# A decoder of two layers on one core: adaLN units moved into layer 1's start and within each mixer's tail, the router's logits copied ahead of the high parts

## The chip, the cores and the metric

The kernel runs on one core of one Trainium2 chip. Its engines are TensorE (PE), VectorE (DVE), ScalarE (ACT), GpSimd (POOL) and SyncE (SP), each with a queue of instructions of its own; SP issues the transfers of the weights. The metric is the device time of one execution in microseconds.

## The reference

A trunk of two layers over 256 tokens of 1024 channels, in f32. Each layer is a token mixer and a mixture of experts, both modulated by adaLN from one conditioning vector `c`:

```python
c_act = jax.nn.silu(c)
for l in range(DEPTH):                                   # 2
    mod = c_act @ ada_w[l] + ada_b[l]                    # (1024) @ (1024 x 6144)
    sh1, sc1, g1, sh2, sc2, g2 = split(mod, 6)
    h = rmsnorm(x, norm_mix_g[l]) * (1 + sc1) + sh1
    proj = h @ w_in[l]                                   # heads of three groups: A, B, C
    oa = differential_attention(...)                     # 4 heads, causal, dense
    ob = banded_attention(..., sink)                     # 8 query heads, window 128
    oc = dilated_mixture(...)                            # 4 heads, three dilations
    x = x + g1 * (concat(oa, ob, oc) @ w_out[l])
    h = rmsnorm(x, norm_ffn_g[l]) * (1 + sc2) + sh2
    x = x + g2 * hierarchical_moe(h, ...)                # best of 4 groups, best 2 of its 4 experts
return rmsnorm(x, final_norm_g)
```

The router's logits are `h @ wg` (4 groups) and `h @ we` (16 experts). An expert is `silu(t @ w_gate) * (t @ w_up)`, weighted, `@ w_down`, with 512 inner channels.

## The kernel before

All 256 tokens stay in SBUF as two tiles `x[0]`, `x[1]` of 128 tokens. What is large is the weights, some 280 MB in all, and they pass through the core once. The class `Ring` holds a ring of 128x1024 tiles (`big`, 512 KB each, and some lent ones, `w` and `k`); `Ring.load` (L154) issues the transfers on SP's queue in one fixed order, which is the order in which TensorE will use them. When the ring is full, the next load waits until the tile that it goes into has been used.

**Order of the work.** TensorE runs its instructions in the order in which the program writes them. The other engines' queues are ordered by a scheduler, which can move an instruction ahead of another one where data and buffers allow; `tc.issue_after` names an instruction that has to come first in the queue. The program's order of a mixer comes from three lists of words, `START`, `MIX` and `TAIL`. `START[l]` is run by `start(l)`, of which layer 1's part is woven into the last expert products of layer 0; `MIX[l]` with `TAIL` at its end is run by `mixer(l)`; then come `router(l)` and `moe(l)`. The words are:

- `X`, `X0` to `X3`: columns of x as it becomes final, transposed (L669). `R`: the inverse norm, as a row product (L680). `S00` to `S02`: splits of the first w_in tiles.
- `P00` to `P43`: pieces of the input projection, each of which uses one w_in tile. An f32 product is made of three products of parts (L718, L719, L720), the high part by ScalarE (L770) and the low part by VectorE (L775), some steps ahead.
- `a`, `c`, `d`, `e`: units of adaLN, a product of `c` and two tiles of `ada_w`. A unit `a` (`ada_unit`, L457, 4 matmuls) belongs to the mixer's shift, scale and gate and the experts' shift (in layer 1, eight units for the last two), a unit `d` or `e` (`one_unit`, L532) to the two halves of what follows the router: four `d` for the second scale, four `e` for the second gate. A unit only adds to a PSUM bank that is read when the last unit is done; what follows it (columns through L475 or L546) is run at the next `flush`.
- `AT AF AV AO AM`, `BT BF BV BO`, `CT CF CV CO`: transposes, scores, values and outputs of the three groups of heads. `CF0` and `CF1` (scores of C, L1074) give their bank to VectorE, which takes the maxima (L829), then ScalarE the exponentials (L835). `CT0` and `CT1` make keys and queries of C (L803; copies L1067 and L1068).
- `W0` to `W6`: output projection, k tile by k tile (`W6` takes the last two), into four banks `acc[t, hf]`. After `W6`, VectorE multiplies by the gate and adds to x (L1141, L1142).

**Router.** `router(l)` transposes x (L803, copies L1180 and L1182), forms raw logits (L1189), has ScalarE copy them (L1195) and adds up their parts (L1196). The inverse norm comes from VectorE's Newton steps (L652 to L660); L1209 multiplies the logits by it. From there VectorE ranks (L1217 to L1229), three small products count places (L1233 to L1235), and L1303 makes the selection matrix `w`. ScalarE scales x to a high part `xhi` (L1206), VectorE forms the low part `xlo` (L1246).

**Experts.** `moe(l)` takes the experts by pairs. `gather` (L1327) collects the chosen tokens by products of `xhi` and `xlo` with the selection matrix; L1361 is the first products (gate and up), L1407 and L1442 the second, L1428 and L1459 the way back to the tokens. A second path of the program, taken when an expert has too many tokens, isn't executed here.

Of the kernel before, what the change touches and what calls it, by code (L numbers as in the profile page):

```python
# [13 lines left out]
AF = mybir.ActivationFunctionType  # L14
# [41 lines left out]

START = ["X c c R c c S00".split(), "S00 S01 X0 X1 S02 X2 X3 a a R".split()]
TAIL = """
CT0 CT1 d d d d CF0 AM1 CF1
W0 BV0 BV1 W1 BV2 BV3 BO0 BV4 W2 BV5 CV0 W3 BO1 CV1 CV2 W4 CO0 W5 W6  # L60
"""
# [6 lines left out]
P00 P01 P02 P03 P10 P11 AT0 P12 AT1 P13 AF0  # L68
P20 a AF1 P21 a AF2 P22 a P23 a
P30 AV0 P31 AV1 a AO0 BT0 P32 AV2 BT1 AO1 P33 AO2 BF0 a  # L70
# [129 lines left out]
class Body:  # L200
# [694 lines left out]
    def mixer(self, l):  # L895
# [221 lines left out]

        def wout(k, t):
            if k == 0 and t == 0:
                for tt in range(2):  # L1120
                    for hf in range(2):
                        acc[tt, hf] = self.acc.tile([128, 512], F32, name="acc")
            self.split_upto(l, 20 + k + AHEAD)
            mix, i = (T["mixa"], k) if k < 2 else (T["mixb"], k - 2) if k < 6 else (T["mixc"], k - 6)
            for hf in range(2):
                self.product(acc[t, hf], [m[:, i, blk(t)] for m in mix],
                             [p[:, 512 * hf:512 * hf + 512] for p in self.parts[20 + k]], k == 0, k == KT - 1)

        def w(k):
            if k < 6:  # L1130
                for t in range(2):
                    wout(k, t)
                return
            self.new_squares()
            for t in range(2):
                for k in (6, 7):
                    wout(k, t)
                for hf in range(2):
                    c = slice(512 * hf, 512 * hf + 512)
                    d = self.w()  # L1140
                    nc.vector.tensor_tensor(out=d, in0=acc[t, hf], in1=mod[l, 2][:, c], op=OP.mult)  # L1141
                    nc.vector.tensor_tensor(out=self.x[t][:, c], in0=self.x[t][:, c], in1=d, op=OP.add)  # L1142
                    self.square(t, hf, 512 * hf, 512 * hf + 512)
# [27 lines left out]
    def router(self, l, dense):  # L1171
        nc, small = self.nc, self.one
# [13 lines left out]
        for t in range(2):  # L1186
            for i in range(2):
                for j in range(4):
                    nc.tensor.matmul(ps[32 * j:32 * j + 32, 128 * t:128 * t + 128], lhsT=self.wrs[:, 4 * i + j],  # L1189
                                     rhs=xt[t, i][:, j], start=(i == 0), stop=(i == 1))  # L1190
        self.common(l, "e")
        pl = [ps[:, 256 + 20 * t:276 + 20 * t] for t in range(2)]
        for t in range(2):
            lt = self.w()[:, 0:128]
            nc.scalar.copy(lt, ps[:, 128 * t:128 * t + 128])  # L1195
            nc.tensor.matmul(pl[t], lhsT=lt, rhs=self.cb[:, C_SEL:C_SEL + 20], start=True, stop=True)  # L1196
        self.common(l, "e")
        r = self.rstds(self.squares())
        if not dense:

            self.xhi, self.xlo = [[self.wk.tile([128, KT, 128], F32R, name="k") for t in range(2)] for _ in range(2)]
            xk = [self.x[t].rearrange("p (k c) -> p k c", k=KT) for t in range(2)]
            for i in range(2):
                for t in range(2):
                    c = slice(4 * i, 4 * i + 4)
                    nc.scalar.activation(self.xhi[t][:, c], xk[t][:, c], AF.Copy, scale=r[t])  # L1206
        lg = small.tile([128, 2, 20], F32, name="lg")
# [101 lines left out]
    def moe(self, l):  # L1309
# [5 lines left out]
        def gather(b, k2):  # L1315
# [7 lines left out]
            for kk in range(2):  # L1323
                n = 0
                for t in range(2):
                    for part in (self.xhi, self.xlo):
                        nc.tensor.matmul(p[:, kk], lhsT=part[t][:, 2 * k2 + kk], rhs=one[:, t],  # L1327
# [323 lines left out]
```

## Time and profile before

| | |
|---|---|
| time, median of 3 runs | 758.12 us (757.98 to 759.51) |
| the profiled execution: its time | 756.71 us |
| its span in the trace | 754.8 us |
| PE busy | 712.9 us (94%) |
| DVE busy | 342.6 us (45%) |
| ACT busy | 211.7 us (28%) |
| moved by DMA | 283.63 MB, 376 GB/s over the span |
| share of the chain that ended last | PE 84%, DVE 8%, ACT 3%, DMA 2% |

How to read it: the span is from the first to the last instruction that the profiler shows, and the execution takes 1.9 us more. Busy shares are means over stages that differ, so what a stage waits for is read from its own stretch of the trace. In rows of the timeline a number in brackets is how long the engine was idle ahead of that row, and behind the arrow stands what ended that. Rows of f32 matmuls count two for each matmul. The granted clock of TensorE is 1.00 at 2.4 GHz and 0.50 at 1.2 GHz.

### The profile page before, as it was taken

Reading aid. Unit: us, or ns where it says so; the run is one execution under the profiler, and the core shown is the slowest. Engines: PE = TensorE matmul, PEld = TensorE weight load, DVE = VectorE, ACT = ScalarE, POOL = GpSimd, SP = SyncE. Lnnn points to the kernel's source line nnn. Section 1 sums busy time; section 2 is a strip of 40 time slices with the busy share of each in tenths; the row PEclk is TensorE's granted clock in tenths of the full one; section 3 lists DMA queues with packets and bytes.
Section 4 is the critical chain, followed back from the end, with each engine's and each line's share of the span. In section 5 each row is a group of like instructions: output and inputs, shape, how many; then the busy total and the mean of one; then the engine's idle time right before and its main releaser. Section 6 shows DMA issues by size and latency. Waiting matters only on the chain.

```text
span 754.8 us, 10672 instructions
## 1 busy us (share of the span) xinstructions
PE 712.9 (94%) x3790; PEld 372.4 (49%) x3790; DVE 342.6 (45%) x940; ACT 211.7 (28%) x482; POOL 65.7 (9%) x89
## 2 busy tenths in 40 slices
PE   6899898999999999999989999897999999999993
PEld 2565675754353353353346668675435335344341
DVE  4587697354042333133357869637213313332234
ACT  2345345432021111111134645643211111112011
POOL 1010234001000000000001121500100000000002
PEclk9899999998999999999989999998999999999997
DMA  9999999998989999999999996879799999999991
GB/s 354 409 409 407 407 409 409 408 379 330 382 336 409 409 410 409 409 409 410 400 406 408 406 404 211 339 241 393 278 363 373 409 409 409 409 410 409 409 382 63
DMA packets 82745, 283.63 MB, mean 376 GB/s; under 512 B 9198, under 2 KB 9327, under 8 KB 82684
## 3 DMA queue, kind: packets, MB, share of 16 engines
q1 hardware_dynamic: 82186, 282.33, 95.6%
q8 instruction: 32, 0.52, 0.3%
q10 hardware_dynamic: 434, 0.53, 0.2%
q14 instruction: 29, 0.24, 0.1%
q0 software_dynamic: 64, 0.02, 0.0%
HBM read 281.78 MB, written 1.06 MB: 375 GB/s over the span
## 4 chain that ended last, share of the span: by engine, by line
PE 84%; DVE 8%; ACT 3%; DMA 2%; issue 1%; SPq 0%; DVEq 0%; ACTq 0%
PE s L1361 30%; PE acc L1407 13%; PE acc L718 6%; PE acc L719 5%; PE acc L720 5%; PE t L1327 5%; PE acc L1428 4%; PE t L803 3%; PE acc L457 3%; DVE k L775 2%; PE acc L1442 2%; DMA big<-in_w_in_dram 1%; PE acc L1459 1%; DMA big<-in_ada_w_first_dram 1%; PE s L884 1%
## 5 line engine op out<-in xcount | busy, mean ns | idle before, releaser
L1361 PE MATMUL s<-big,k 128*64 128x512 f32 x976 | 228.2, 598 | 0.0
L1361 PEld LDWEIGHTS s<-big,k 128*64 128x64 f32 x976 | 67.4, 136 | 118.6 <-issue 104.8
L1413 DVE SCALAR_TENSOR_TENSOR w<-acc,gs,g 128x512 f32<-128x512 f32 x28 | 21.0, 751 | 155.3 <-PE acc L1407 153.8
L1407 PE MATMUL acc<-big,w 128*64 128x512 f32 x384 | 84.4, 592 | 0.0
L718 PE MATMUL acc<-k 128*128 128x512 f32 (+1 forms) x176 | 69.8, 397 | 3.8 <-ACT k L707 3.6
L775 DVE TENSOR_TENSOR k<-big,k 128x1024 fp32r<-128x1024 f32 (+1 forms) x56 | 66.0, 1186 | 15.7 <-ACT k L770 11.4
L720 PE MATMUL acc<-k 128*128 128x512 f32 (+1 forms) x176 | 66.8, 380 | 0.0
L719 PE MATMUL acc<-k 128*128 128x512 f32 (+1 forms) x176 | 66.3, 377 | 0.0
L770 ACT CAST k<-big 128x1024 fp32r<-128x1024 f32 (+1 forms) x56 | 53.9, 985 | 35.0 <-PE acc L719 26.8
L1407 PEld LDWEIGHTS acc<-big,w 128*64 128x64 f32 x384 | 27.6, 137 | 54.8 <-issue 52.8
L1392 DVE TENSOR_TENSOR w<-w,s 128x512 f32<-128x512 f32 x16 | 11.0, 688 | 84.3 <-PE s L1361 84.3
L718 PEld LDWEIGHTS acc<-k 128*128 128x128 f32 x176 | 33.6, 191 | 19.8 <-issue 7.3
L1327 PEld LDWEIGHTS t<-w,k 128*128 128x128 f32 x256 | 35.4, 205 | 16.0 <-issue 8.1
L1417 ACT CAST w<-w 128x512 fp32r<-128x512 f32 x28 | 17.3, 619 | 89.6 <-DVE w L1413 89.6
L835 ACT ACTIVATE w<-w,nm 128x128 f32<-128x128 f32 (+1 forms) x80 | 35.4, 445 | 22.4 <-DVE nm L833 20.2
L1327 PE MATMUL t<-w,k 128*128 128x256 f32 x256 | 39.8, 306 | 1.8 <-DVE w L1303 1.5
L724 ACT ACTIVATE k<-t,mod,mod 128x256 f32<-128x256 f32 x32 | 16.3, 561 | 85.4 <-PE t L1327 85.4
L1398 ACT COPY w<-t 128x512 f32<-128x512 f32 x16 | 9.4, 586 | 107.9 <-PE t L803 107.9
L720 PEld LDWEIGHTS acc<-k 128*128 128x128 f32 x176 | 33.7, 191 | 8.0 <-DVE k L891 1.6
L719 PEld LDWEIGHTS acc<-k 128*128 128x128 f32 x176 | 33.8, 192 | 4.9
L803 PE MATMUL t<-cb,w 128*128 128x128 f32 x224 | 33.6, 278 | 2.0 <-ACT w L860 0.7
L1430 DVE TENSOR_TENSOR x<-x,acc 128x512 f32<-128x512 f32 x56 | 34.9, 682 | 0.2
(269 smaller groups left out, 857.1 us busy)
## 6 DMA issues: line engine op xcount, KB each, us to landing
big<-in_expert_w_up_dram SPq DMA_DIRECT2D x126, 512.0 KB, 10.2
big<-in_expert_w_gate_dram SPq DMA_DIRECT2D x118, 512.0 KB, 10.2
big<-in_expert_w_down_dram SPq DMA_DIRECT2D x108, 512.0 KB, 10.2
big<-in_ada_w_dram SPq DMA_DIRECT2D x80, 512.0 KB, 10.2
big<-in_w_in_dram SPq DMA_DIRECT2D x32, 512.0 KB, 10.2
big<-in_ada_w_first_dram SPq DMA_DIRECT2D x16, 512.0 KB, 10.2
big<-in_w_out_dram SPq DMA_DIRECT2D x16, 512.0 KB, 9.0
w<-in_expert_w_down_dram SPq DMA_DIRECT2D x20, 256.0 KB, 7.4
```

What stands on the lines that cost most here:

```text
L718: self.nc.tensor.matmul(p, lhsT=xh, rhs=wh, start=start, stop=False)
L719: self.nc.tensor.matmul(p, lhsT=xh, rhs=wl, start=False, stop=False)
L720: self.nc.tensor.matmul(p, lhsT=xl, rhs=wh, start=False, stop=stop)
L770: nc.scalar.copy(hi, w)
L775: nc.vector.tensor_tensor(out=lo, in0=w, in1=hi.bitcast(F32), op=OP.subtract)
L803: self.nc.tensor.transpose(p[:, i], b, self.ident)
L835: nc.scalar.activation(e[:, h], e[:, h], AF.Exp, bias=nm[:, g:g + 1], scale=scale, accum_out=sm[:, g:g + 1])
L1327: nc.tensor.matmul(p[:, kk], lhsT=part[t][:, 2 * k2 + kk], rhs=one[:, t], start=(n == 0), stop=(n == 3))
L1361: nc.tensor.matmul(store[j][64 * u:64 * u + 64, :], lhsT=x[k // 4][:, k % 4, c:c + 64], rhs=w[u][kk], start=(k == 0), stop=(k == KT - 1))
L1407: nc.tensor.matmul(ps[hf][64 * u:64 * u + 64, :], lhsT=act[j][:, f, 64 * u:64 * u + 64], rhs=w[u][hf], start=(f == 0), stop=(f == 3))
L1428: nc.tensor.matmul(p, lhsT=pts[j][:, 128 * t:128 * t + 128], rhs=part, start=(n == 0), stop=(n == 1))
L1430: nc.vector.tensor_tensor(out=self.x[t][:, c], in0=self.x[t][:, c], in1=p, op=OP.add)
```

## The change

Five parts, of which the first two are lists of words.

1. `START[1]` has five units `a` instead of two, one behind X1, one behind X2, two behind X3 and one behind `R`. Three units fewer stand in `MIX[1]` among P20 to P23.
2. `TAIL`, used by both layers, has its four units `d` apart: one behind each of CT0 and CT1, two behind AM1. `W0` is ahead of CF1.
3. In `W6` of both layers the two k tiles are finished for one half of the columns, then for the other.
4. In `router` the copies of the logits and their product stand ahead of the two last units `e`, and `issue_after` puts the high parts behind the copies in ScalarE's queue.
5. In `gather` the products of the high part stand ahead of those of the low part.

```diff
-START = ["X c c R c c S00".split(), "S00 S01 X0 X1 S02 X2 X3 a a R".split()]
+START = ["X c c R c c S00".split(), "S00 S01 X0 X1 a S02 X2 a X3 a a R a".split()]
 TAIL = """
-CT0 CT1 d d d d CF0 AM1 CF1
-W0 BV0 BV1 W1 BV2 BV3 BO0 BV4 W2 BV5 CV0 W3 BO1 CV1 CV2 W4 CO0 W5 W6
+CT0 d CT1 d CF0 AM1 d d W0 CF1
+BV0 BV1 W1 BV2 BV3 BO0 BV4 W2 BV5 CV0 W3 BO1 CV1 CV2 W4 CO0 W5 W6
 """
...
-P20 a AF1 P21 a AF2 P22 a P23 a
+P20 AF1 P21 a AF2 P22 P23
...
-        def wout(k, t):
+        def wout(k, t, hfs=(0, 1)):
...
-            for hf in range(2):
+            for hf in hfs:
...
             for t in range(2):
-                for k in (6, 7):
-                    wout(k, t)
                 for hf in range(2):
+                    for k in (6, 7):
+                        wout(k, t, (hf,))
...
-        self.common(l, "e")
         pl = [ps[:, 256 + 20 * t:276 + 20 * t] for t in range(2)]
         for t in range(2):
             lt = self.w()[:, 0:128]
-            nc.scalar.copy(lt, ps[:, 128 * t:128 * t + 128])
+            copied = nc.scalar.copy(lt, ps[:, 128 * t:128 * t + 128])
             nc.tensor.matmul(pl[t], lhsT=lt, rhs=self.cb[:, C_SEL:C_SEL + 20], start=True, stop=True)
+        self.common(l, "e")
         self.common(l, "e")
...
-            for i in range(2):
-                for t in range(2):
-                    c = slice(4 * i, 4 * i + 4)
-                    nc.scalar.activation(self.xhi[t][:, c], xk[t][:, c], AF.Copy, scale=r[t])
+            with self.tc.issue_after(copied.ins):
+                for i in range(2):
+                    for t in range(2):
+                        c = slice(4 * i, 4 * i + 4)
+                        nc.scalar.activation(self.xhi[t][:, c], xk[t][:, c], AF.Copy, scale=r[t])
...
-                for t in range(2):
-                    for part in (self.xhi, self.xlo):
+                for part in (self.xhi, self.xlo):
+                    for t in range(2):
```

The changed file has one line more from `router` on, so that L1196 of before is L1195 there, L1206 is L1207, and L1459 is L1460.

On TensorE in the tail of layer 0 (L803 are transposes, L532 the units `d`, L1074 the scores of C, L718 and its like W0):

```order
 L457 MATMUL acc<-big,cb 32x512 x16
-L803 MATMUL t<-cb,w 128x128 x8
-L532 MATMUL acc<-big,cb 32x512 x16
+L803 MATMUL t<-cb,w 128x128 x4
+L532 MATMUL acc<-big,cb 32x512 x4
+L803 MATMUL t<-cb,w 128x128 x4
+L532 MATMUL acc<-big,cb 32x512 x4
 L1074 MATMUL s<-w 128x128 x4
 L803 MATMUL t<-cb,w 128x128 x2
-L1074 MATMUL s<-w 128x256 x4
+L532 MATMUL acc<-big,cb 32x512 x8
```

Two units stand ahead of CF0 instead of four, and two behind AM1 where CF1 stood. CF1 itself comes twelve matmuls and two steps later, ahead of BV0:

```order
 L475 MATMUL t<-cb,w 128x128 x4
 L546 MATMUL t<-cb,w 128x2 x4
+L1074 MATMUL s<-w 128x256 x4
 L803 MATMUL t<-cb,w 128x128 x8
```

L475 and L546 are the columns of the `a` and `d` units, which run at W0's `flush`.

On ScalarE in the router (L1206, or L1207 after, are the high parts; L1195, or L1194 after, the copies of the logits), before and after:

```order
L1206 ACTIVATE k<-x,newton 128x512 x2
L1195 COPY w<-s 128x128
L1206 ACTIVATE k<-x,newton 128x512 x2
L1195 COPY w<-s 128x128
```

```order
L1194 COPY w<-s 128x128 x2
L1207 ACTIVATE k<-x,newton 128x512 x4
```

The two copies are side by side now, and all four high parts behind them. On TensorE, the product of the copies follows L1189 at once, with the last two units `e` behind it.

On TensorE at the start of layer 1 (L669 are X0 to X3, L457 the units `a`, L680 is `R`, L1459, or L1460 after, the last expert products of layer 0, and L718 the first matmul of P00), before and after:

```order
L669 MATMUL t<-cb,x 128x128 x4
L669 MATMUL s<-cb,x 128x128 x4
L1459 MATMUL acc<-w 128x256 x2
L669 MATMUL t<-cb,x 128x128 x4
L1459 MATMUL acc<-w 128x256 x2
L669 MATMUL s<-cb,x 128x128 x4
L457 MATMUL acc<-big,cb 32x512 x8
L680 MATMUL acc<-w,ones 128x128 x2
L718 MATMUL acc<-k 128x512
```

```order
L669 MATMUL t<-cb,x 128x128 x4
L669 MATMUL s<-cb,x 128x128 x4
L457 MATMUL acc<-big,cb 32x512 x4
L1460 MATMUL acc<-w 128x256 x2
L669 MATMUL t<-cb,x 128x128 x4
L457 MATMUL acc<-big,cb 32x512 x4
L1460 MATMUL acc<-w 128x256 x2
L669 MATMUL s<-cb,x 128x128 x4
L457 MATMUL acc<-big,cb 32x512 x8
L680 MATMUL acc<-w,ones 128x128 x2
L457 MATMUL acc<-big,cb 32x512 x4
L718 MATMUL acc<-k 128x512
```

A unit now stands ahead of each of the last two expert products, and one between `R` and P00. The loads follow, on SP (each row is so many loads of 512 KB):

```order
-L154 DMA big<-in_w_in_dram 128x1024 x3
-L154 DMA big<-in_ada_w_dram 128x1024 x4
-L154 DMA big<-in_w_in_dram 128x1024 x8
...
+L154 DMA big<-in_w_in_dram 128x1024 x2
+L154 DMA big<-in_ada_w_dram 128x1024 x2
+L154 DMA big<-in_w_in_dram 128x1024
+L154 DMA big<-in_ada_w_dram 128x1024 x8
+L154 DMA big<-in_w_in_dram 128x1024 x9
```

Ten ada_w loads now lie among the layer's first thirteen, where four lay among the first seven and then none up to the fifteenth.

## Rows read from the trace of the kernel before

**Rows 1.** The page: GB/s in 40 equal slices of the span.

```profile
GB/s 354 409 409 407 407 409 409 408 379 330 382 336 409 409 410 409 409 409 410 400 406 408 406 404 211 339 241 393 278 363 373 409 409 409 409 410 409 409 382 63
```

**Rows 2.** Stretches: busy us (instructions) by engine; last: granted clock, DMA share, GB/s.

```profile
150.00:220.00 70.00, 66.63 (x369) 33.37 (x369) 27.46 (x77) 15.53 (x33) 2.72 (x12) 0.95 0.93 352
220.00:350.00 130.00, 130.00 (x637) 53.43 (x635) 35.19 (x67) 18.89 (x37) 0.00 (x0) 1.00 1.03 409
...
450.00:570.00 120.00, 113.35 (x698) 69.54 (x699) 62.21 (x209) 46.28 (x115) 15.68 (x23) 0.97 0.83 305
...
124.00:127.40 3.40, 3.40 (x10) 2.63 (x9) 2.64 (x14) 2.30 (x11) 1.28 (x3) 0.50 1.02 405
...
526.00:530.20 4.20, 4.01 (x16) 3.56 (x16) 4.20 (x14) 1.22 (x3) 0.20 (x1) 0.51 0.87 339
```

**Rows 3.** Waits of SP, the load queue: total us, times, longest.

```profile
SPq L154 <- PE s L1361: 81.5, 59, 7.7
```

**Rows 4.** Timeline of PE, tail of layer 0 (start, us, what [idle before]).

```profile
119.66 0.72 PE L1074 MATMUL s<-w 64*128 64x128 f32 x8
...
122.23 1.46 PE L1074 MATMUL s<-w 64*128 64x256 f32 x8 [1.48 <-DVE mx L829]
123.62 0.52 PE L718 MATMUL acc<-k,w 128*128 128x512 f32 x1
...
128.06 0.60 PE L475 MATMUL t<-cb,w 128*128 128x128 f32 x4
...
130.57 0.66 PE L803 MATMUL t<-cb,w 128*128 128x128 f32 x4 [0.57 <-DVE mod L550]
```

**Rows 5.** Timeline of DVE there.

```profile
118.28 0.71 DVE L1068 COPY w<-t 128x256 f32<-128x256 f32 x2
...
120.44 1.23 DVE L775 TENSOR_TENSOR k<-big,k 128x1024 fp32r<-128x1024 f32 x1
```

**Rows 6.** Timeline of PE, tail of layer 1.

```profile
479.44 1.46 PE L1074 MATMUL s<-w 64*128 64x256 f32 x8 [1.32 <-ACT w L1050]
480.82 0.50 PE L718 MATMUL acc<-k,w 128*128 128x512 f32 x1
...
483.69 0.95 PE L546 MATMUL t<-cb,w 128*128 128x2 f32 x8
```

**Rows 7.** Timeline of PE, router of layer 1.

```profile
516.91 0.66 PE L803 MATMUL acc<-cb,x 128*128 128x128 f32 x4 [0.27 <-DVE x L1142]
...
522.17 0.40 PE L1196 MATMUL s<-cb,w 128*128 128x20 f32 x2 [0.98 <-ACT w L1195]
...
526.77 3.54 PE L1327 MATMUL t<-w,k 128*128 128x256 f32 x15 [0.15 <-DVE k L1246]
```

**Rows 8.** Timeline of ACT, router of layer 1.

```profile
520.63 1.33 ACT L1206 ACTIVATE k<-x,newton 128x512 fp32r<-128x512 f32 x2
```

**Rows 9.** Timeline of DVE, router of layer 1.

```profile
520.25 0.21 DVE L660 TENSOR_SCALAR newton<-newton 128x1 f32<-128x1 f32 x1
522.61 0.39 DVE L1209 SCALAR_TENSOR_TENSOR lg<-s,newton,rbias 128x20 f32<-128x20 f32 x2 [2.14 <-PE s L1196]
```

**Rows 10.** Waits of PE, whole kernel: total us, times, longest.

```profile
PE s L1196 <- ACT w L1195: 3.0, 4, 1.0
```

**Rows 11.** Timeline of PE, a later gather in layer 0's experts.

```profile
218.47 2.07 PE L1327 MATMUL t<-w,k 128*128 128x256 f32 x16
```

**Rows 12.** Timeline of PE, start of layer 1; last, an a unit in P20.

```profile
394.40 3.20 PE L457 MATMUL acc<-big,cb 128*32 128x512 f32 x16
...
399.77 0.50 PE L718 MATMUL acc<-k 128*128 128x512 f32 x1 [1.52 <-ACT k L707]
...
426.89 1.06 PE L457 MATMUL acc<-big,cb 128*32 128x512 f32 x8
```

**Rows 13.** Timeline of SP: loads in the order issued.

```profile
383.02 9.29 SPq L154 DMA_DIRECT2D big<-in_w_in_dram  x8
```

**Rows 14.** The page, DMA issues: queue, count, KB each, median us to landing.

```profile
big<-in_ada_w_dram SPq DMA_DIRECT2D x80, 512.0 KB, 10.2
```

## The prediction

> **What bounds the kernel now.** I began with the line of the page that gives GB/s in 40 slices [rows 1]. The reader is to see a flat 406 to 410 with two dents, around slices 9 to 12 and slices 24 to 30. So the stream of weights is at its ceiling nearly everywhere, and time can be won only where it dents, or at the two ends. The view by stretches [rows 2] puts sizes to that. At 409 GB/s the stretch 150 to 220 us, which moved 352, stood still for 70 x (409 - 352) / 409 = 9.8 us; the stretch 450 to 570, which moved 305, for 120 x (409 - 305) / 409 = 30.5 us. Each is the end of a token mixer, a router and the first experts. What stopped the stream there is in SP's waits [rows 3]: the load queue was held 81.5 us by matmuls of the experts' first products (L1361), because the ring was full and a buffer comes free only as TensorE eats it. In those two dents TensorE's chain sets the time. From 220 to 350 TensorE is busy 130.00 of 130 us [rows 2] while the stream is full too: it works off the full ring, and each layer's end is close to a tie of both.
>
> From that follows how a saving is paid out. What TensorE gains ahead of a layer's first L1361 releases the ring earlier by the same time and shortens the dent. It is kept up to the dent's length, 9.8 and 30.5 us, and the gains of the two layers add. A gain in transfers would be worth nothing there. So each edit is priced by what it takes out of TensorE's sequence, waits included, ahead of L1361.
>
> **1. The tail of layer 0.** Before [rows 4], CF1's scores waited 1.48 us for a maximum by VectorE, which stood behind a split L775 of 1.23 us [rows 5]. W0's twelve rows ran from 123.62 to 128.06, 4.44 us, and the stretch 124.0 to 127.4 had a granted clock of 0.50 [rows 2], the lower level of 1.2 GHz; TensorE had just had that wait. The same W0 in layer 1 took 480.82 to 483.69, 2.87 us [rows 6]; so the low clock cost 1.57. Then BV1 waited 0.57. These three are 3.62 us that are no work. After, two d units and the whole of W0, nearly 5 us, stand between AM1 and CF1, so the maximum is there long before, and CF1 stands between L546 and BV0, so VectorE has time for what BV1 waited for. What is late next is CF0: two of the four d units, about 0.9 us each, no longer stand ahead of it. It began at 119.66 [rows 4], and TensorE would reach it at about 117.9; but its keys come by the first of the two copies L1068, which start at 118.28 and take 0.71 together [rows 5], so at 118.63: 0.7 lost. The d units and their loads stay the same in number and cost. Sum -2.9. Bounds: -3.6 without the new wait; -1.0 if CF0 waits a microsecond behind other VectorE work and the clock falls all the same (-3.62 + 1.0 + 1.57). I take -2.9, since the stretch that ended in the low clock is now filled with work.
>
> **2. The tail of layer 1.** The wait before CF1 is 1.32 us [rows 6], for ScalarE, and W0 is at full clock already. VectorE and ScalarE are behind TensorE here, so I let most of the wait move ahead of CF0: -0.3, bounds -1.0 and +0.5.
>
> **3. The router, in both layers.** In layer 1 the second product of the logits (L1196) waits 0.98 us for ScalarE's copy [rows 7], because ScalarE's queue holds two high-part activations ahead of it, 1.33 us [rows 8]. VectorE's L1209 then starts at 522.61, after an idle of 2.14 us [rows 9]. It also needs the inverse norm, whose last step ends at 520.25 + 0.21 = 520.46 [rows 9]. After, the logits are copied straight behind L1189 and are ready about then, so the norm is what comes last: -2.1. The high parts follow the copies on ScalarE: four of 0.67 us from about 520.1 end at 522.8. The gather that reads them ran its main part from 526.77 [rows 7] and its first row 0.7 earlier; moved up by 2.5 us that first row stands at 523.5. That covers them by 0.7; a longer ScalarE queue is paid one to one beyond it. The two e units behind the logits, about 1.0 us each, lie in the 4 us between L1209 and the gather. W6's order finishes the first half of its second tile three matmuls earlier, 0.7 us by W0's twelve in 2.87 [rows 6], but TensorE waited there only 0.27 [rows 7]: -0.3. Both high products ahead of the low ones in the gather let L1246's result come a matmul or two later; the wait for it is 0.15 [rows 7]: -0.2. Sum -2.6 a layer. That layer 0 has the same shape is seen in TensorE's waits: four waits of L1196 for ScalarE, 3.0 us together [rows 10], so 1.5 a layer.
>
> Bounds: the gather's last 15 rows ran 3.54 us [rows 7] at a granted clock of 0.51 [rows 2], where 16 of them took 2.07 later in the kernel [rows 11]. If with the waits gone the clock stays up, 1.4 us more is won: -4.0. If the stretch at 1.2 GHz comes later against the work, so that L1361 begins in it, I let as much be lost: -1.2. I leave it at -2.6, as both before and after TensorE waits some 2 us for VectorE here.
>
> **4. Five a units in START of layer 1.** Three of them leave P20 to P23, 1.06 us each at full clock [rows 12], 1.0 without what the next row overlaps: -3.0. A copy's time, 0.35 as in [rows 5], I take back for VectorE, which the units gave time there. In START they stand in waits that exist, of which 1.52 us before P00 is the last [rows 12]. But they need their loads earlier. A tile of 512 KB at 409 GB/s lands every 1.28 us, and the page has 10.2 us from issue to landing [rows 14]. The fifth unit now ends on the thirteenth load of the layer. That is the sixth of the eight issued from 383.02 [rows 13]: issued at 389.4, there at about 399.6 to 400. Half a unit hangs on its second tile, so P00 starts no earlier than about 400.5, against 399.77 [rows 12]: +0.7, net -1.9. At half clock two units took 3.20 us [rows 12] instead of 2.1; if all run so, the norm shifts too, and P00 comes at about 402.4: net 0. I take the middle, P00 at 401.4: -1.0. The worst bound has three projection pieces at half clock besides, +3.4. Eight a loads ahead of the rest of w_in put its fourth tile six places back, at about 401, needed for the fourth piece at about 408: hidden.
>
> **Sum.** Layer 0: -2.9 - 2.6 = -5.5, within its 9.8. Layer 1: -1.0 - 0.3 - 2.6 = -3.9. Together -9.4. The profiled execution took 756.71 us (span 754.8); 756.71 - 9.4 = 747.3, span 745.4. The median of the runs shown is 1.4 above the profiled one, so 748.7.
>
> **The rivals.** *The router alone* pays: the tail's wait goes to CF0 entirely and START gains nothing. 2 x -2.6 = -5.2, 752.9. For it: VectorE is what TensorE waits for in the tail [rows 4]. Against: 1.57 us of the tail is clock, not waiting.
>
> *The transfers set the time.* If the stream could not follow an earlier release, layer 0's 5.5 us would be waited for at its end, and only layer 1's 3.9 remains: 754.2. For it: 409 GB/s through the experts [rows 1, 2]. Against: 81.5 us in which the queue waited for TensorE [rows 3]. The Trainium skill, Perfetto Trace Analysis, section Roofline, puts a lone core's ceiling at some 435 GB/s from its 16 DMA engines. By that rule the stream is the roof in the flat slices, and the trace agrees, with 409 to 410 there, but not in the dents.
>
> *The clock goes against it* (slower). The units in START each wait for a tile, with TensorE idle in between; if the granted clock stays at 1.2 GHz into the projection, the same matmuls take twice as long. Each microsecond of work so stretched costs one: from P00 at 401 on, the 9.4 are eaten when 18.8 us more are spent at half clock, until about 420; beyond that the kernel is slower, and until 425 it is at 760.6. For it: two units there took 3.20 us [rows 12]. Against: P00's first matmul took 0.50 [rows 12] and no more, although it came behind such waits. The Trainium skill, TensorE: Matmul & The Clock Gate, section HAM oscillation — how this bites in real kernels, speaks for this case: short groups of matmuls parted by waits for data start slow each time. The trace agrees for the two units, not for P00.
>
> *The clock goes for it*: the gather at full clock in both layers, -1.4 each, and START at -1.9: 745.0.
>
> *The norm is late*: if other work on VectorE goes ahead of it, L1209 waits for it instead, and I put the router at -1.3 a layer, half: 751.3.
>
> **Chances.** The forecast 0.45, router alone 0.15, norm late 0.12, clock for it 0.10, transfers 0.08, clock against it 0.10 (half of it at or near 420, half beyond). The range goes from 744.5, a bit below the good clock, to 754.5, which takes in the transfers' case. Faster by over 0.2% (1.5 us, about what a measurement of this kernel can tell): all but the clock against it, and 0.02 of the transfers' case, 0.88; within 0.2% 0.07; slower 0.05.
>
> **What would show it.** L1209 without the idle of 2.14 us, its releaser the norm; ScalarE's two copies side by side; no wait of 1.48 before CF1 in layer 0 but some 0.7 before CF0; W0 there in 2.9 us; L1361 5.5 us earlier in layer 0 and 9.4 in layer 1; the first dent shorter; P00 between 400.5 and 402.4, less layer 0's 5.5. Wrong would be: L1361 earlier in layer 0 but layer 1's P00 not (transfers); stretches at 0.5 that are longer than before; VectorE at L1209 waiting for the logits still.

## The result, and the profile after

The changed kernel takes 750.8 us (median of 4 runs, 750.01 to 751.72), beside it the kernel before 758.82 (4 runs, 757.98 to 759.73). The ratio is 0.9895, with a 95% interval of 0.9874 to 0.9916: 1.0% faster, 8.0 us of medians, where 9.4 and 748.7 were forecast. The profiled execution took 750.05 us with a span of 748.3, against 756.71 and 754.8.

The page's GB/s in 40 slices, of the changed kernel:

```profile
GB/s 352 409 410 406 406 410 408 408 386 409 391 357 409 409 410 409 408 409 410 397 408 409 406 406 210 335 209 401 327 339 396 409 409 409 409 409 409 409 379 63
```

Against [rows 1] the first dent (slices 9 to 12) is nearly gone, the second is as deep as it was. The view by stretches has the sizes (columns as in [rows 2]):

```profile
150.00:220.00 70.00, 67.43 (x378) 33.16 (x378) 28.65 (x79) 17.04 (x36) 2.71 (x12) 1.00 0.99 384
...
450.00:570.00 120.00, 114.69 (x697) 67.35 (x696) 62.53 (x203) 44.41 (x112) 15.48 (x23) 0.99 0.83 309
...
470.00:475.00 5.00, 4.38 (x27) 1.44 (x27) 3.73 (x21) 4.43 (x20) 0.00 (x0) 0.70 0.94 329
...
167.00:171.00 4.00, 3.17 (x18) 2.37 (x20) 3.95 (x11) 1.02 (x2) 0.00 (x0) 1.00 1.03 411
...
520.00:524.00 4.00, 3.26 (x20) 2.38 (x22) 3.97 (x11) 1.02 (x2) 0.00 (x0) 1.00 1.02 405
```

From 150 to 220 us it moved 384 GB/s instead of 352, so the stream stood still for 70 x (409 - 384) / 409 = 4.3 us instead of 9.8. The 5.5 us between them are near the time by which TensorE came to the experts sooner in layer 0, which by the first L1361 (now L1362) is 175.64 - 170.59 = 5.05 us. From 450 to 570 it is 309 after 305: there TensorE won little more. Layer 1's first L1361 comes 530.24 - 523.51 = 6.73 us sooner, where 9.4 were forecast. The last three rows are of the granted clock: 0.70 in layer 1's tail, 1.00 in both first gathers, where [rows 2] had 0.51 in layer 1. SP's waits for the experts' first products, 81.5 us in [rows 3], are 76.7 now.

**The tail of layer 0.** Timeline of PE (start, us, what, idle before):

```profile
119.55 0.71 PE L1074 MATMUL s<-w 64*128 64x128 f32 x8 [0.40 <-DVE w L1068]
...
120.56 1.92 PE L532 MATMUL acc<-big,cb 128*32 128x512 f32 x16
122.41 0.50 PE L718 MATMUL acc<-k,w 128*128 128x512 f32 x1
...
125.27 0.60 PE L475 MATMUL t<-cb,w 128*128 128x128 f32 x4
...
126.59 1.13 PE L1074 MATMUL s<-w 64*128 64x256 f32 x8
```

The wait of 1.48 for a maximum and that of 0.57 [rows 4] are gone, and W0's twelve rows take 122.41 to 125.27, 2.86 us instead of 4.44. What is late instead is CF0, by 0.40. CT0 itself stands 0.84 us later than before, and that comes from further ahead, where the code is the same: from the scores of B on, the stage is 3.33 us shorter. At 82.9 us the changed kernel was still some 0.5 us ahead of the one before, but then its granted clock fell to 0.50, where the kernel before has 1.00 in the same stretch:

```profile
82.90:86.30 3.40, 3.40 (x13) 2.92 (x11) 0.73 (x2) 0.59 (x1) 0.00 (x0) 0.50 1.02 408
```

**The router.** Timelines of PE, DVE and ACT in layer 1:

```profile
514.52 1.06 PE L1189 MATMUL s<-w,wrs 128*32 128x128 f32 x32
516.01 0.40 PE L1195 MATMUL s<-cb,w 128*128 128x20 f32 x2 [0.44 <-ACT w L1194]
516.77 0.40 PE L1195 MATMUL s<-cb,w 128*128 128x20 f32 x2 [0.35 <-ACT w L1194]
...
520.73 2.85 PE L1328 MATMUL t<-w,k 128*128 128x256 f32 x16 [0.83 <-DVE w L1304]
523.51 1.94 PE L1362 MATMUL s<-big,k 128*64 128x512 f32 x8
```

```profile
516.39 0.21 DVE L660 TENSOR_SCALAR newton<-newton 128x1 f32<-128x1 f32 x1
517.21 0.39 DVE L1210 SCALAR_TENSOR_TENSOR lg<-s,newton,rbias 128x20 f32<-128x20 f32 x2 [0.60 <-PE s L1195]
```

```profile
516.45 0.27 ACT L1194 COPY w<-s 128x128 f32<-128x128 f32 x1 [0.49 <-PE s L1195]
```

VectorE's L1210 (L1209 before) no longer idles for 2.14 us [rows 9], but still for 0.60, and what ends that is PE's second product, not the norm, which was there at 516.39 + 0.21 = 516.60. So it still waits for the logits, which the prediction had named as a sign of being wrong. On ScalarE the second copy waits 0.49 us for the first product, and PE's second product 0.35 for that copy: the four go one after the other. The gather then takes 520.73 to 523.51, 2.8 us instead of some 4.2 [rows 7].

**The tail of layer 1.** Timeline of PE:

```profile
470.62 0.72 PE L1074 MATMUL s<-w 64*128 64x128 f32 x8 [1.80 <-DVE w L1068]
...
471.64 3.31 PE L532 MATMUL acc<-big,cb 128*32 128x512 f32 x16
474.88 0.75 PE L718 MATMUL acc<-k,w 128*128 128x512 f32 x1
...
484.92 1.09 PE L803 MATMUL t<-cb,w 128*128 128x128 f32 x8 [0.68 <-ACT w L860]
```

The wait of 1.32 ahead of CF1 [rows 6], and one of 0.64 for VectorE ahead of CT1 that the prediction passed over, have become one of 1.80 ahead of CF0. Behind it the two d units take 3.31 us, where two in layer 0 took 1.92, and W0's first row took 0.75, where in layer 0 it took 0.50: the granted clock fell here. And a wait of 0.68 for ScalarE, which the kernel before did not have, stands behind W1.

**The start of layer 1.** Timeline of PE from the last products of layer 0 (L1460) to P00 (L718), and the weight loads' wait there:

```profile
376.97 1.98 PE L1460 MATMUL acc<-w 128*128 128x512 f32 x4
...
381.79 2.14 PE L457 MATMUL acc<-big,cb 128*32 128x512 f32 x8
...
386.36 1.41 PE L457 MATMUL acc<-big,cb 128*32 128x512 f32 x8
...
390.20 2.67 PE L457 MATMUL acc<-big,cb 128*32 128x512 f32 x16
...
393.45 1.97 PE L457 MATMUL acc<-big,cb 128*32 128x512 f32 x8
395.36 0.50 PE L718 MATMUL acc<-k 128*128 128x512 f32 x1
```

```profile
PEld acc L457 <- DMA big<-in_ada_w_dram: 2.9, 5, 0.9
```

The five units (L457) waited 2.9 us for their tiles. P00 comes 395.36 - 376.97 = 18.4 us after L1460 of 512 columns, where before it came 399.77 [rows 12] - 382.16 = 17.6 after it; that row before:

```profile
382.16 1.98 PE L1459 MATMUL acc<-w 128*128 128x512 f32 x4
```

In the projection behind P00, with three units fewer, TensorE has two waits for VectorE that it did not have before, 1.04 us together:

```profile
422.71 1.94 PE L984 MATMUL s<-k,w 64*128 64x512 f32 x4 [0.33 <-DVE mx L829]
...
437.44 0.47 PE L718 MATMUL acc<-k 128*128 128x512 f32 x1 [0.71 <-DVE w L792]
```

### The profile page after: what moved, and what is told of

Same layout as the page of the kernel before. It is cut to its first block, busy times and chain, and to the rows that moved or that the text cites. A ratio compares the mean times of both kernels' runs of the same rounds, so it can differ in the third digit from the quotient of the medians.

```text
span 748.3 us, 10676 instructions
## 1 busy us (share of the span) xinstructions
PE 711.3 (95%) x3790; PEld 368.8 (49%) x3790; DVE 342.1 (46%) x940; ACT 211.5 (28%) x482; POOL 65.3 (9%) x89
## 3 DMA queue, kind: packets, MB, share of 16 engines
HBM read 281.78 MB, written 1.06 MB: 378 GB/s over the span
## 5 line engine op out<-in xcount | busy, mean ns | idle before, releaser
L1362 PE MATMUL s<-big,k 128*64 128x512 f32 x976 | 228.2, 598 | 0.0
L1362 PEld LDWEIGHTS s<-big,k 128*64 128x64 f32 x976 | 67.4, 136 | 118.5 <-issue 103.2
L718 PE MATMUL acc<-k 128*128 128x512 f32 (+1 forms) x176 | 70.0, 397 | 3.0 <-ACT k L707 2.0
L718 PEld LDWEIGHTS acc<-k 128*128 128x128 f32 x176 | 33.9, 193 | 18.2 <-issue 6.1
L1328 PEld LDWEIGHTS t<-w,k 128*128 128x128 f32 x256 | 32.8, 190 | 16.3 <-issue 9.9
L1328 PE MATMUL t<-w,k 128*128 128x256 f32 x256 | 37.6, 291 | 1.7 <-DVE w L1304 1.7
L803 PE MATMUL t<-cb,w 128*128 128x128 f32 x224 | 34.1, 281 | 1.4 <-ACT w L860 1.4
```

Source lines behind the costliest of these rows:

```text
L718: self.nc.tensor.matmul(p, lhsT=xh, rhs=wh, start=start, stop=False)
L803: self.nc.tensor.transpose(p[:, i], b, self.ident)
L1362: nc.tensor.matmul(store[j][64 * u:64 * u + 64, :], lhsT=x[k // 4][:, k % 4, c:c + 64], rhs=w[u][kk], start=(k == 0), stop=(k == KT - 1))
```

## The experiments

For each run I read from PE's timeline the same eight starts, and so seven stages: layer 0's tail (from the last scores of B ahead of CT0 to W1), the router of layer 0 (from L1189 to the first L1361), the start of layer 1 (from L1459 of 512 columns to P00), its projection (P00 to the last scores of B), its tail (from there to W1), its output (W1 to L1189) and its router. Lines are those of before. Microseconds, each the difference of two starts:

| run | tail 0 | router 0 | start 1 | projection 1 | tail 1 | output 1 | router 1 | ratio to before (95%) |
|---|---|---|---|---|---|---|---|---|
| before | 20.55 | 11.57 | 17.61 | 70.77 | 14.79 | 33.04 | 11.87 | 1 |
| changed | 17.22 | 8.99 | 18.39 | 69.16 | 16.25 | 33.75 | 8.99 | 0.9895 (0.9874 to 0.9916) |
| start_alone | 20.54 | 11.89 | 18.35 | 69.16 | 14.78 | 33.11 | 11.89 | 1.0 (0.9985 to 1.0015) |
| tail_alone | 17.22 | 11.88 | 15.23 | 72.32 | 16.27 | 33.88 | 11.87 | 0.9938 (0.9917 to 0.996) |
| router_alone | 20.56 | 10.33 | 15.23 | 72.25 | 14.78 | 33.12 | 8.99 | 0.9904 (0.9872 to 0.9936) |
| tail1_old | 17.24 | 8.99 | 19.15 | 69.20 | 14.81 | 33.07 | 8.99 | 0.987 (0.9848 to 0.9892) |
| tail1_w0 | 17.22 | 10.23 | 18.40 | 69.13 | 13.88 | 34.41 | 8.96 | 0.988 (0.9856 to 0.9903) |
| one_copy | 17.22 | 9.53 | 18.40 | 69.22 | 14.59 | 33.52 | 8.65 | 0.9896 (0.9871 to 0.9921) |
| gather_old | 17.22 | 8.98 | 18.75 | 69.17 | 16.25 | 34.02 | 9.79 | one run, 750.33 us |
| w6_old | 17.22 | 10.32 | 18.38 | 69.14 | 16.21 | 33.98 | 10.10 | one run, 751.5 us |
| tail1_filled | 17.23 | 10.32 | 18.06 | 69.14 | 18.94 | 33.09 | 9.00 | 0.9921 (0.9906 to 0.9936) |
| best_old_start | 17.23 | 8.65 | 15.24 | 72.28 | 16.35 | 33.12 | 8.66 | 0.9882 (0.9865 to 0.9899) |
| best_four | 17.23 | 9.98 | 15.92 | 69.47 | 14.78 | 33.12 | 9.05 | 0.9822 (0.9806 to 0.9838) |

The stages, from the profiled execution of each run, are of three kinds. Layer 0's tail follows the list of words within 0.1 us (20.55 or 17.22). The start of layer 1 with five units lies anywhere from 18.06 to 19.15 with no low clock in it, and that goes with the wait of its units for their tiles, 2.5 us in the run with 18.06 and 4.2 in the run with 19.15. And what the granted clock sets comes and goes: a router with the first gather at 1.2 GHz is some 1.3 us longer than the same one without, and a list can't be judged by a stage in which only one of two runs had a low clock.

### start_alone

```diff
-START = [..., "S00 S01 X0 X1 S02 X2 X3 a a R".split()]
+START = [..., "S00 S01 X0 X1 a S02 X2 a X3 a a R a".split()]
-P20 a AF1 P21 a AF2 P22 a P23 a
+P20 AF1 P21 a AF2 P22 P23
```

> Only the START and P20 to P23 lists of the change. Theory A (the forecast's term): three units leave the mixer, P00 comes 0.7 to 1.6 us later, net -1.0, about 0.9987 of before; P00 begins 0.7 to 1.6 us after 399.77 as counted from the end of layer 0. Rival: the units wait for their loads and P00 comes 2.6 us later, so nothing is won (0 to -0.3). Second rival: with the clock kept up by the added work, -1.9 or more.

The time does not move: 757.98 us by 12 runs, 757.95 before by 17. Start and projection together are 87.51 us here and 87.55 in the changed kernel; with the old lists 88.38 in the profile of before, 87.55 in tail_alone and 87.48 in router_alone. So nothing is won, as in the first rival, but not for its reason alone. All four profiles with the old START have a stretch at 1.2 GHz behind its waits, now in START itself (before, 17.61 us, [rows 12]), now in the first pieces of the projection (72.3 us instead of 70.77). The eight with five units and best_four have none there. Without that stretch the old start is 15.23 us, so the units cost 3.2 us in it and give back 1.6 in the projection; the other 1.6 is the clock, which stayed up in the nine profiles with four or five units and fell in the four with two. What the waits are without them shows in router_alone, in PE's timeline:

```profile
389.19 0.66 PE L669 MATMUL t<-cb,x 128*128 128x128 f32 x4 [1.75 <-DVE x L1467]
...
391.49 0.66 PE L669 MATMUL s<-cb,x 128*128 128x128 f32 x4 [0.78 <-DVE x L1467]
...
394.72 0.68 PE L680 MATMUL acc<-w,ones 128*128 128x128 f32 x4 [0.72 <-DVE w L679]
396.92 0.52 PE L718 MATMUL acc<-k 128*128 128x512 f32 x1 [1.52 <-ACT k L707]
```

With the old list X2 and X3 wait 1.75 and 0.78 us for x, and the norm's row (L680) waits 0.72. A unit ahead of X2 or X3 that takes longer than what it covers pushes back the whole chain from x to the norm and P00: X3 comes 9.80 us after the expert products of 512 columns here and 12.64 in the changed kernel, which is 2.84 of the 3.2.

### tail_alone

```diff
-CT0 CT1 d d d d CF0 AM1 CF1
-W0 BV0 BV1 W1 BV2 BV3 BO0 BV4 W2 BV5 CV0 W3 BO1 CV1 CV2 W4 CO0 W5 W6
+CT0 d CT1 d CF0 AM1 d d W0 CF1
+BV0 BV1 W1 BV2 BV3 BO0 BV4 W2 BV5 CV0 W3 BO1 CV1 CV2 W4 CO0 W5 W6
```

> Only the TAIL list, in both layers. The forecast's terms: -2.9 in layer 0 and -0.3 in layer 1, -3.2 together (0.9958). Theory B, from the trace of the changed kernel: -3.3 in layer 0, but layer 1 loses, since a wait of 1.8 us ahead of CF0 takes TensorE to 1.2 GHz for the d units (1.4 to 1.75 us) and a later wait for ScalarE of 0.7 comes up: -3.3 + 2.2 = -1.1 (0.9985). By B, W1 in layer 1 stands later against the last CT0 there than in the kernel before; by A it does not.

753.67 us, ratio 0.9938, so some 4.3 us by medians: more than either theory, with an interval (0.4% to 0.8%, 3.0 to 6.3 us) that takes in the forecast's 3.2. B's sum of -1.1 lies outside that interval. In the profile B's stages are there: layer 0's tail is 3.33 shorter, to the hundredth as in the changed kernel, and layer 1's tail and output are 1.5 and 0.8 longer. But the profiled execution took 756.74 us, the longest of the six, at a mean granted clock of 0.975 where the other five have 0.978. So the gain in layer 0 is shown, and the loss in layer 1 is shown for this execution, not for the others. The start of layer 1 had its low clock later in this profile, which is not the list's doing.

### router_alone

```diff
-        self.common(l, "e")
...
-            nc.scalar.copy(lt, ps[:, 128 * t:128 * t + 128])
+            copied = nc.scalar.copy(lt, ps[:, 128 * t:128 * t + 128])
...
+        self.common(l, "e")
         self.common(l, "e")
...
+            with self.tc.issue_after(copied.ins):
```

and the orders of W6 and of the gather.

> Only W6's order, the logits and the gather's order, in both layers. The forecast: -2.6 a layer, -5.2 (0.9931), with the logits' copies alone worth 2.1 of 2.6. Theory B, from the changed kernel's trace: the sum is the same, -2.6 to -2.9 a layer, but the logits are worth 1.5 and the rest is TensorE at 2.4 GHz in the first gather; then a run in which the clock falls there again has only -1.5 a layer (-3.0).

Ratio 0.9904, 5.7 us by medians, as forecast. Router 1 is 2.88 shorter with the first gather at full clock, router 0 with a partly slow one only 1.24. L1189 to the first gather row is 7.67 us before and 6.2 in every kernel with the two copies of this part, 1.45 a layer less. B holds.

### tail1_old and tail1_w0

Both are the changed kernel with a list of its own for layer 1's tail:

```diff
-""" + TAIL).split()]
+""" + TAIL1).split()]
...
+TAIL1 (tail1_old) = CT0 CT1 d d d d CF0 AM1 CF1 W0 BV0 BV1 W1 ...
+TAIL1 (tail1_w0)  = CT0 CT1 d d d d CF0 AM1 W0 CF1 BV0 BV1 W1 ...
```

> The changed kernel, with layer 1's tail as it was before. Theory B (the change cost layer 1's tail about 2 us): 2 us faster than the changed kernel, ratio to before about 0.987, and no stretch at 1.2 GHz there. Theory A (that tail is worth -0.3): 0.3 us slower than the changed kernel, 0.990.

747.89 us, 2.9 below the changed kernel's median in another set of runs. By the ratios to before it is 1.9 (0.987 and 0.9895), and their intervals overlap, so the times alone don't settle it. Tail and output of layer 1 are 47.88 us together, 50.00 in the changed kernel: 2.1, as B has it, for the two profiled executions.

> The changed kernel, with all four d units ahead of CF0 in layer 1 as before, and only W0 moved ahead of CF1 there. Theory: CF0 then finds its keys, W0's 2.9 us hide the wait of 1.32 for CF1, and nothing makes the clock fall: from the last BF2 scores to W1 some 13.4 us, against 14.8 with the old tail and 16.25 with the changed one, so 2.8 us faster than the changed kernel, and 0.7 of that more in the wait for ScalarE behind W1. Rival: CF1's wait comes back at BV0 or at W1 (ScalarE is late by itself), and it takes 14.8 as before.

The tail is 13.88, but the output is 34.41, so both together are 48.29, 0.4 more than with the old list: the rival holds. In PE's timeline the time comes back behind W1:

```profile
482.85 1.10 PE L807 MATMUL t<-cb,w 128*128 128x128 f32 x8 [1.38 <-ACT w L864]
```

With the old list no such wait is there. What TensorE is ahead it has to give back to ScalarE: the wait ends with ScalarE's copy of transposed probabilities (L864, L860 in the kernel before). Why that copy does not come sooner is open.

### one_copy

```diff
+        lts = self.w()[:, 0:256]
+        copied = nc.scalar.copy(lts, ps[:, 0:256])
         for t in range(2):
-            lt = self.w()[:, 0:128]
-            copied = nc.scalar.copy(lt, ps[:, 128 * t:128 * t + 128])
-            nc.tensor.matmul(pl[t], lhsT=lt, ...)
+            nc.tensor.matmul(pl[t], lhsT=lts[:, 128 * t:128 * t + 128], ...)
```

> The changed kernel, with the logits of both token tiles copied by one instruction of 256 columns and the two products behind it. Theory A: the logits are late because the second copy waits for the first product, which writes the same PSUM tile, so that copy, product, copy, product go one after the other; then VectorE's L1210 waits for the norm and the first gather comes about 0.6 us sooner after L1189 in each layer (5.6 instead of 6.21), 1.2 us in all. Rival: the norm or the high parts are what come last; then it stays at 6.1 to 6.2 and the time does not change.

L1189 to the first gather row is 5.86 in both layers, 0.35 less than in the changed kernel, where 0.6 was expected; the time, 749.68 us, can't tell that. VectorE's timeline in layer 1:

```profile
516.71 0.21 DVE L660 TENSOR_SCALAR newton<-newton 128x1 f32<-128x1 f32 x1
517.19 0.39 DVE L1210 SCALAR_TENSOR_TENSOR lg<-s,newton,rbias 128x20 f32<-128x20 f32 x2 [0.26 <-PE s L1195]
```

The second wait is gone, but L1210 still waits 0.26 us for the product behind a norm that ends at 516.92. The theory holds with half its size.

This run has more to say on layer 1's tail. PE's timeline there, and the stretch's clock:

```profile
472.82 0.71 PE L1074 MATMUL s<-w 64*128 64x128 f32 x8 [1.79 <-DVE w L1068]
...
473.84 1.92 PE L532 MATMUL acc<-big,cb 128*32 128x512 f32 x16
475.69 0.50 PE L718 MATMUL acc<-k,w 128*128 128x512 f32 x1
```

```profile
472.00:476.00 4.00, 3.17 (x27) 1.44 (x28) 3.98 (x22) 3.53 (x15) 0.00 (x0) 1.00 0.67 254
```

The list is that of the changed kernel and the wait ahead of CF0 is the same, 1.79 us. But the clock stayed at 1.00, two d units took 1.92 us instead of 3.31, and the tail 14.59 instead of 16.25. So up to W1 the list alone takes 0.2 less than the old one, and 1.66 us are the clock. With the output behind it, which holds the wait for ScalarE, it is 14.59 + 33.52 = 48.11 us where before it was 47.83: even with the clock up this list wins nothing in layer 1.

### gather_old and w6_old

```diff
-                for part in (self.xhi, self.xlo):
-                    for t in range(2):
+                for t in range(2):
+                    for part in (self.xhi, self.xlo):
```

> The changed kernel, with the old order in the gather. The forecast's term: 0.2 us later from the first gather row to L1362 (3.0 instead of 2.78). Rival: no difference, since VectorE's low parts come one every 0.41 us and set the gather's end in either order.

In layer 0, where the clock is as in the changed kernel, first gather row to L1362 is 2.77 us, and 2.78 there:

```profile
166.22 0.36 PE L1328 MATMUL t<-w,k 128*128 128x256 f32 x1 [0.83 <-DVE w L1304]
166.86 2.21 PE L1328 MATMUL t<-w,k 128*128 128x256 f32 x15 [0.28 <-DVE k L1247]
```

The wait of 0.28 that the old order has is inside the new one's rows. The rival holds, and the term is nil: in both kernels VectorE's eight low parts (L1247) start 0.1 us after the first gather row and take 3.25 us, 0.41 each.

```diff
-                for hf in range(2):
-                    for k in (6, 7):
-                        wout(k, t, (hf,))
+                for k in (6, 7):
+                    wout(k, t)
+                for hf in range(2):
```

> The changed kernel, with W6's old order. The forecast's term: the wait of 0.27 for x is removed by the change, so it would be here and not in the changed kernel; the changed kernel has 0.26 still, so the rival is no difference from W6 to L1189, and VectorE's last Newton step up to 1 us later, hidden or not behind the logits (0.6 us of room).

The wait for x is the same, 0.26, with either order, and W1 to L1189 in layer 0 is 33.10 in both:

```profile
513.20 0.66 PE L803 MATMUL acc<-cb,x 128*128 128x128 f32 x4 [0.26 <-DVE x L1142]
```

This term is nil too. Both runs are single executions, read by these stages and not by their times.

### tail1_filled

```diff
+        def fill(n):
+            p = acc[0, 0] = self.acc.tile([128, 512], F32, name="acc")
+            for i in range(7):
+                nc.tensor.matmul(p, lhsT=self.ident, rhs=self.cb[:, 0:512], start=True, stop=True)
...
+TAIL1 = CT0 d CT1 d MM0 CF0 AM1 d d W0 CF1 ...
```

> The changed kernel, with seven products of 128x512 that nobody reads put ahead of CF0 in layer 1's tail, where TensorE waits 1.8 us for its keys; their bank is overwritten by W0 later. It does more work. Theory (the granted clock is what this tail lost): with the wait filled the clock stays up, the d units behind AM1 take 1.9 us instead of 3.31, W0's first row 0.4 instead of 0.75, and from the last BF2 scores to W1 it is 14.6 to 14.9 us instead of 16.25; 1.4 to 1.7 us faster than the changed kernel in that stretch, though the products are added. Rival: the d units are slow there by their loads or by VectorE's traffic; then they stay at 3.3, and the stretch at 16.2 or longer.

Timeline of PE in layer 1's tail:

```profile
468.44 6.28 PE L1153 MATMUL acc<-cb 128*128 128x512 f32 x14
474.65 0.72 PE L1078 MATMUL s<-w 64*128 64x128 f32 x8
...
475.66 1.92 PE L536 MATMUL acc<-big,cb 128*32 128x512 f32 x16
477.51 0.50 PE L722 MATMUL acc<-k,w 128*128 128x512 f32 x1
```

The seven products took 6.2 us, not the 1.8 that I had meant, so the kernel is slower than the changed one. What was to be seen is behind them: the d units take 1.92 and W0's first row 0.50. Without the products' 6.21 the tail is 12.73; the changed one without its wait of 1.80 is 14.45, and the 1.7 between them are the clock again. One profile with the wait filled shows little of what keeps the clock up, since one_copy kept it with the wait open. The expectation's rival is out by other rows: in the changed kernel the units wait for no tile of ada_w there, and single rows of their matmuls take up to 1.06 us, where they take 0.59 to 0.62 in one_copy with the same order.

### best_four and best_old_start

Both have tail1_old and one_copy. best_old_start has START and P20 to P23 as before the change; best_four has

```diff
+START = [..., "S00 S01 X0 X1 S02 X2 X3 a a a R a".split()]
+P20 AF1 P21 a AF2 P22 a P23
```

> The changed kernel with three edits: layer 1's old tail, the logits copied by one instruction, and four units in START behind X3 and R (X3 a a a R a) instead of five, the fourth put back behind P22. Theory for START: units ahead of X2 and X3 delay the chain from X3 over the norm to P00 by their full length, units behind X3 lie in the norm's time; then from the last 512 columns of the expert products (L1459) to P00 it is 15.3 to 15.8 us (18.4 in the changed kernel), and from there to BF2 about 69.7 (69.2): 2 to 2.6 us less than in the changed kernel. With the tail (2.1) and the logits (0.7): about 745.5, 0.9835 of before. Rival: P00 is set by the loads; then it is 17 or more.

> As best_four, but with START and P20 to P23 as they were before the change. Theory: START is worth nothing, so 748 or a little less, 0.987, with 15.2 to 17.6 us to P00 by where the clock falls, and 70.7 to 72.3 from there to BF2. If the five units were worth the forecast's 1.0, it is 1 us slower than the changed kernel with the same two edits.

best_four is the fastest kernel here: 745.02 us, 0.9822 of before, an interval clear of the changed kernel's. Start and projection are 15.92 + 69.47 = 85.39, 2.2 less than in the changed kernel. PE's timeline at the start of layer 1:

```profile
376.61 1.98 PE L1464 MATMUL acc<-w 128*128 128x512 f32 x4
...
384.11 0.66 PE L673 MATMUL t<-cb,x 128*128 128x128 f32 x4 [1.75 <-DVE x L1471]
...
386.41 0.66 PE L673 MATMUL s<-cb,x 128*128 128x128 f32 x4 [0.78 <-DVE x L1471]
387.00 3.04 PE L461 MATMUL acc<-big,cb 128*32 128x512 f32 x24
...
390.60 2.00 PE L461 MATMUL acc<-big,cb 128*32 128x512 f32 x8
392.53 0.50 PE L722 MATMUL acc<-k 128*128 128x512 f32 x1
```

X2 and X3 wait as with the old list, three units lie in the norm's time, and P00 comes right behind the fourth, which takes 2.00 us because it waits 0.8 for its tile. best_old_start has 87.52 for the two stages, as the five units have; that START is worth nothing is confirmed, and four units in other places, with the clock up as with the five, are worth 2.1 by the two stages and 3.2 by the medians of the two kernels, whose intervals are clear of each other. Its tail 1 took 16.35 us with the old list, at a granted clock of 0.66:

```profile
472.00:477.00 5.00, 5.00 (x19) 3.77 (x18) 3.68 (x15) 2.76 (x13) 4.34 (x5) 0.66 1.03 417
```

So in that place the old list can lose the clock as well.

## Why the prediction was right

The sum held, -6.7 us in the two profiled executions and -8.0 by medians for -9.4, but its terms did so in part only, and that they add up so well is partly luck: a loss in layer 1's tail that was not foreseen, and a START worth nothing, stand against a router whose logits gave less and whose clock gave more.

| term | forecast | measured |
|---|---|---|
| tail, layer 0 | -2.9 | -3.33 |
| router, layer 0 | -2.6 | -2.58 |
| START and P20 to P23 | -1.0 | -0.83 in the two profiles, 0.0 by itself |
| tail, layer 1 | -0.3 | +2.17 |
| router, layer 1 | -2.6 | -2.88 |
| ahead of layer 0's tail, where nothing is changed | none | +0.84 |

The measured terms are differences of stages of the two profiled executions. Run by themselves, START, the tails and the router gained 0.0, 4.3 and 5.7 us by medians, 10.0 in all where the changed kernel has 8.0; with intervals of 1 to 2.5 us to either side of each, that is no shown difference. The +0.84 comes with the low clock at 82.9 us, not with the change.

**How savings are paid out** was right: L1361 of layer 0 comes 5.05 us sooner, and the last products of that layer 5.19 sooner. The transfers followed, and the dent is 5.5 us shorter. The rival by which the transfers set the time is out.

**Layer 0's tail** was right in each step: the clock's 1.57 and both waits are won back. Only the new wait ahead of CF0 is 0.40 instead of 0.7. The clock's part is the list's doing as far as thirteen profiles can show it: W0 of layer 0 ran at a granted clock of 1.00 in all ten with the new list, and of 0.63 to 0.66 in all three with the old one.

**The router** had the right sum of wrong parts. The logits were taken at -2.1, up to the norm; they are -1.45, since two copies and two products that share a PSUM tile go one after the other, and the norm is there 0.6 us ahead of the last of them. one_copy shows 0.35 of that; in it the product still comes 0.26 behind the norm. The Trainium skill, PSUM — Partial Sum Buffer, section PSUM bank collisions raise a hardware error, has two engines on one bank and quadrant kept apart even at different columns; the trace agrees, with 0.49 and 0.35 us of waiting where copy and product touch different columns of that tile. W6's and the gather's order, -0.3 and -0.2, are nil. What makes up for it is the clock: the first gather ran at 1.00 in both layers, which was a rival's -1.4 a layer. That it did so in both layers of this execution is luck and no sure gain: in the ten profiles with the new router the stretch from the first gather row to L1361 took about 2.8 us in 11 of 20 cases and 3.2 to 4.1 in the others; in the three with the old one it took 3.9 to 4.2 in all six.

**Layer 1's tail** is the step that failed. That VectorE is behind and the wait moves ahead of CF0 was right, and by one_copy's 14.59 so was the size up to W1 (-0.2). But the step let it end there. In the changed kernel the longer wait was followed by 1.2 GHz, 1.66 us, and what TensorE gained beyond that it waited for behind W1, 0.7. -0.2 + 1.66 + 0.7 make up the +2.17 of this execution; without the fall of the clock it is +0.3 (one_copy). The rival by which the clock goes against the change was put into START; it was in the other place. The Trainium skill, TensorE: Matmul & The Clock Gate, section HAM oscillation — how this bites in real kernels, has groups of matmuls behind waits for data start slow. The traces agree for this tail in four of the five profiles that have its list and a wait of about 1.8 us, and not in the fifth, one_copy; with the old list one of six fell. What decides it between executions with equal order is open: the runs show that it varies, not why.

**START** was right in that the units wait for their tiles, 2.9 us, and P00 is 0.8 us later than in the kernel before. That is near the sum's first bound (0.7), where the middle, 1.6, was taken. But the row that it was counted from held a low clock itself; against a start without one they cost 3.2 us, and leaving P20 to P23 gives back 1.6 where 2.65 was forecast, since TensorE waits 1.04 for VectorE there where the sum took off 0.35. That the clock stayed up with the units makes the sum nil. The rival that had them take the clock down was the wrong way round here.

## What to carry to other kernels

A row of one profile that ran at half clock is no baseline: before a saving is counted from it, ask whether the stage has that clock in other executions, and price both. Work that is moved into a wait must have its data before the wait begins, and must not stand ahead of the link that the wait's chain comes from; four units behind X3 won 2 us, five around it nothing. On a list used by two layers, look at each layer for the engine that is behind: the order that freed TensorE in one made it wait twice in the other.

## What the runs showed that I had not expected

Seven f32 products of 128x512 with a stationary tile of 128x128 took 6.2 us at full clock, 0.9 each; four products of a unit of adaLN, each with 32 columns of the stationary tile, took 1.06 together, 0.27 each. I had priced the filler by the latter. But those four run beside each other: in the unit of [rows 12] they start within 0.02 us, where the filler's products start one after the other.

The granted clock fell or stayed in the same place, with the same order and the same wait (1.79 and 1.80 us), from one execution to the next. In most sets of five or more, the runs of one kernel spread by 3 to 6 us (in one set of nine by 2), and the clock goes with it at least in part: in router_alone from 747.66 us at a mean granted clock of 0.989 to 753.73 at 0.980.
